# A hybrid layer and an expert layer on one core: more buffers for the RWKV keys, and TensorE's instructions held to the written order

## The chip, the cores and the metric

One core of a Trainium2 chip runs the whole program once. The metric is the device time of that execution in microseconds (us). TensorE is called PE here, VectorE DVE, ScalarE ACT, GpSimd POOL; SP is the engine that issues nearly all transfers.

## What is computed

Two layers follow each other on 2048 tokens of width 1024. The first is a hybrid layer: one projection `u = rmsnorm(x) @ w_in`, whose columns feed a gated linear attention (GLA, 4 heads) and an RWKV-7 recurrence (8 heads of 64), and one output projection. The second is a short convolution and 16 experts, each over 256 tokens. The change touches the RWKV part alone:

```python
def step(S, inp):                       # one token, per head; S is 64 x 64
    r_t, w_t, k_t, v_t, kk_t, a_t = inp
    sa = jnp.einsum('bhvk,bhk->bhv', S, -kk_t)
    S = (S * w_t[:, :, None, :]
         + sa[..., None] * (kk_t * a_t)[:, :, None, :]
         + v_t[..., None] * k_t[:, :, None, :])
    y = jnp.einsum('bhvk,bhk->bhv', S, r_t)
    return S, y
```

The kernel computes it in chunks of 64 tokens: products inside a chunk, the inverse of a small triangular matrix per head and chunk, and a state that goes from chunk to chunk.

## The kernel before

**The projection sets the pace.** `w_in` is multiplied in pieces of 128 columns by 512 tokens (four blocks of tokens, b = 0 to 3). Each weight and each activation is split in a high and a low part, so that one piece is 24 products of 128x128 by 512 columns (a depth of eight 128s, three products each): `dense` (line 85) issues 12 products, then calls `tick`, then 12 more and `tick` again. Products of this kind are called dense below. A piece of a block whose tokens have just been exchanged is written in two halves of 256 tokens (`proj`, line 356, product at line 384).

**The recurrence is written into the gaps.** `tick` ends a slot: it runs the steps that `plan` holds for that slot. A step is the stretch of a generator between two `yield`s; `yield n` puts the next stretch n slots later, and in a slot the steps of rank 0 come first, then 1, then 2. A block of 256 tokens (blk = 0 to 7) has two calls of `rwkv_prepare` (128 tokens each, 11 slots apart, rank 1) and one of `rwkv_chain` (rank 0, 27 slots after the block's start); blocks start 21 slots apart. There are 236 slots in all.

**`rwkv_prepare`** loads r, k, v, the decays `cs` and the keys' gates `ta` from DRAM. Two slots later it forms the keys `km` (from `ta` and k) and `rk`; three slots later PE sums `sq` and `rk` over each head (lines 1341, 1342, operand `hsel`) and DVE and POOL make the norm `nr`; three slots later the normed keys `kk`, the operands `ar`, and the scaled `ta` and `km`. Then PE turns `km`, `ta` and v token by token into `tks`, `tbs`, `tv` (three slots), and in the last two slots multiplies `ta` and `km` by `ar` (16 small products per chunk and operand pair, tile `rp`); DVE masks the results into `Ak`, `Ab0`, `Ab1`, and SP writes the two 32 x 32 triangles of `Ab0` to DRAM (`Ld`).

**`rwkv_chain`** loads the triangles, one per partition, and solves them on DVE: 31 steps j of two instructions each (lines 1436, 1438, tiles `PR` and `LX`), six steps to a slot. A copy (line 1441) and transfers through DRAM (`Xd`) bring the inverses into `TX` and `TM`; three slots later PE joins the halves (`pu<-TM,Ab`, then `pu<-TM,P`). Then each of four chunks takes three slots: state and values into `px`, `py`; `TX` times `WP` into `pu`; `U` into the state and the output.

**`decays`** (line 474, product at line 489) is the small projection of decays and gates: its first product `rp<-e,up` is written one slot after the piece that makes its operand e. **`modulation`** (line 125) is a side task in four sets of eight loads `araw`, summed by DVE into `acc` and by PE through `ahi`, `alo`. **`start_heads`** runs when all eight chains are written: it writes what is left of the modulation, and from then on two steps of the GLA heads go into each slot.

**What sets the order.** The program is not executed as written: a scheduler replays it with modelled times, gives each engine the oldest written instruction that the model takes as ready, and hands out a tile's buffers as they come free. Each engine then executes its list in that order. `burst` (line 1279) only holds the later products of a group behind its first.

Of the kernel before, what the change touches and what calls it, by code (L numbers as in the profile page):

```python
# [37 lines left out]

def bcast_rows(ap, n):

    return bass.AP(tensor=ap.tensor, offset=ap.offset, ap=[[0, 128], [1, n]])
# [3 lines left out]
def block_kernel(ctx: ExitStack, tc: tile.TileContext, A: dict, out: bass.AP, dbg=None, upto=99):  # L45
    nc = tc.nc
    dbg = dbg or {}
# [37 lines left out]
    def dense(ps, rhs, tick, parts):  # L85

        for k4 in range(0, KD, 4):
            hi, lo = parts()
            for k in range(4):
                rh, rl = rhs(k4 + k)  # L90
                nc.tensor.matmul(ps, hi[:, k, :], rh, start=(k4 + k == 0), stop=False)  # L91
                nc.tensor.matmul(ps, hi[:, k, :], rl, start=False, stop=False)  # L92
                nc.tensor.matmul(ps, lo[:, k, :], rh, start=False, stop=(k4 + k == KD - 1))  # L93
            tick()
# [56 lines left out]
    with ExitStack() as hps:  # L151
# [24 lines left out]
        def over_tokens():  # L176

            nw = rp.tile([1, D], F32, name="nw", tag="ar", bufs=3)
            nc.sync.dma_start(nw, A["norm_w"])
            one = rp.tile([1, 128], F32, name="one", tag="Ak", bufs=6)  # L180
            nc.vector.memset(one, 1.0)
            for c in range(0, D, 512):
                p = pst("mm", [128, 512], 2)
                nc.tensor.matmul(p, one, nw[:, c:c + 512], start=True, stop=True)
                nc.scalar.activation(nw_bc[:, c:c + 512], p, AF.Copy)
# [45 lines left out]
        def turned(tt):  # L231
# [4 lines left out]
            for g in range(2):  # L236
                p = pst("rp", [128, 4, 128], 3)
                for k in range(4):
                    nc.tensor.transpose(p[:, k, :], xr[:, (4 * g + k) * 128:(4 * g + k + 1) * 128], ident)
# [51 lines left out]
        nc.tensor.transpose(pv[:, :nv], vrow, ident[:nv, :nv])  # L291
# [40 lines left out]
        TX = cst.tile([128, 2, 4, 4, 64], F32)  # L332
# [23 lines left out]
        def proj(c0, at=""):  # L356
# [17 lines left out]
            else:  # L374
# [4 lines left out]
                for h in range(2):  # L379
                    hs = slice(h * 256, h * 256 + 256)  # L380
                    for k in range(KD):
                        hi, lo = (t[:, k % 4, :] for t in w[k // 4])
                        for l, r in ((hi, 0), (hi, 1), (lo, 0)):
                            nc.tensor.matmul(ps[:, hs], l, hT[r][:, k, hs], start=(k == 0 and l is hi and r == 0),
# [9 lines left out]
        def pair(c0, after=None):  # L394
# [3 lines left out]
            for k in range(KD):  # L398
# [6 lines left out]
                for o, w in zip(ps, ws):  # L405
                    hi, lo = (t[:, k % 4, :] for t in w)
                    for l, r in ((hi, 0), (hi, 1), (lo, 0)):
                        nc.tensor.matmul(o, l, hT[r][:, k], start=(k == 0 and l is hi and r == 0),
# [65 lines left out]
        def decays(b, e):  # L474
# [7 lines left out]
            for p in range(4):  # L482
# [3 lines left out]
                for i, (l, r) in enumerate(((0, eh), (0, el), (1, eh))):  # L486
                    for g in range(2):
                        rs = slice(64 * g, 64 * g + 64)
                        nc.tensor.matmul(ps[g], up[l][rs, c], r[rs], start=(i == 0), stop=(i == 2))
# [9 lines left out]
        def others(b, starts, after):  # L499
# [19 lines left out]
            for k in range(KD):  # L519
                nc.tensor.matmul(ps[0:32], gw[:, k, :], hT[0][:, k, :], start=(k == 0), stop=False,  # L520
                                 skip_group_check=True)
                nc.tensor.matmul(ps[0:16], gw[:, k, 0:16], hT[1][:, k, :], start=False,
# [21 lines left out]
        def gate_sums(b, ps):  # L544
# [6 lines left out]
            for g in range(2):  # L551
                pz = pst("mm", [128, TB], 2)
                nc.tensor.matmul(pz, gup[:, g * 128:g * 128 + 128], e, start=True, stop=True)
# [744 lines left out]
def rwkv_prepare(nc, blk, q, Ap, L):  # L1298

    rp, pst, ident, vcol = L["rp"], L["pst"], L["ident"], L["vcol"]  # L1300
# [13 lines left out]
    cs, ta = tmp("cs"), tmp("ta")  # L1314
# [15 lines left out]
    km = tmp("km")  # L1330
# [9 lines left out]
    for p in range(4):  # L1340
        nc.tensor.matmul(pn[:, 0, 2 * p:2 * p + 2], sq[:, p, :], hsel, start=True, stop=True)
        nc.tensor.matmul(pn[:, 0, 8 + 2 * p:10 + 2 * p], rk[:, p, :], hsel, start=True,
# [10 lines left out]
    for p in range(4):  # L1353
        nc.tensor.transpose(pb[:, p, :], nb[:, p, :], ident)
# [13 lines left out]
    for nme, s in (("ks", km), ("bs", ta), ("v", v)):  # L1368
        yield 2 if nme == "ks" else 1
        pT = pst("rp", T4, 3)  # L1370
        for p in range(4):
            nc.tensor.transpose(pT[:, p, :], s[:, p, :], ident)
        for c in range(2):
            tok[nme, c] = tmp("t" + nme, [128, 4, 64], 6)
# [4 lines left out]
        if nme == "v":  # L1379

            bo = tmp("bo", [128, 512], 3)
# [5 lines left out]
    for c in range(2):  # L1387
# [10 lines left out]
        burst(nc, L["tc"], products)  # L1398
        ent = {}
        ent["Ak"] = tmp("Ak", T4, 6)  # L1400
        nc.vector.tensor_mul(ent["Ak"], pA[0], amask[:, None, :].to_broadcast(T4))
        for a, bufs in ((0, 4), (1, 6)):
            ent["Ab" + str(a)] = tmp("Ab" + str(a), [128, 4, 64], bufs)
            cs_ = slice(64 * a, 64 * a + 64)
            nc.vector.tensor_mul(ent["Ab" + str(a)], pA[1][:, :, cs_],
                                 amask[:, None, cs_].to_broadcast([128, 4, 64]))
        for h in range(2):
            for bl in range(2):
                o = (1 - h) * 64 + bl * 32
                nc.sync.dma_start(Ld[blk % 2, bl, 2 * q + c, :, h].rearrange("p s t -> s p t"),  # L1410
                                  ent["Ab0"][o:o + 32, :, bl * 32:bl * 32 + 32])
# [4 lines left out]
def rwkv_chain(nc, blk, Ap, L):  # L1416

    rp, pst = L["rp"], L["pst"]
    S, TX, Ld, Xd = (L[n] for n in ("S", "TX", "Ld", "Xd"))
    orow, rsqrt, dbg, lnw_bc, tc = (L[n] for n in ("orow", "rsqrt", "dbg", "lnw_bc", "tc"))  # L1420
    T4 = [128, 4, 128]
    tmp, scr = rwkv_tiles(rp)
    TT = TX[:, blk % 2]
# [9 lines left out]
    for j in range(31):  # L1433
# [5 lines left out]
        if j % 6 == 5:  # L1439
# [30 lines left out]
    for c in reversed(range(4)):  # L1470
        for p in range(4):
            for o in (0, 64):
                products.append(((pP[o + 32:o + 64, c, p, :], Ap[c]["Ab0"][o:o + 32, p, 32:64],
                                  TM1(o)[:, :, 4 * c + p, :].rearrange("i o m -> i m o")),
                                 dict(start=True, stop=True)))
    burst(nc, tc, products)
# [13 lines left out]
    burst(nc, tc, products)  # L1490
# [7 lines left out]
    for c in range(4):  # L1498
# [13 lines left out]
        burst(nc, tc, products)  # L1512
# [12 lines left out]
        burst(nc, tc, products)  # L1525
# [4 lines left out]
        for p in range(4):  # L1530
            for o, w in ((pS, e["bs"]), (py, e["Ab1"])):
# [4 lines left out]
        burst(nc, tc, products)  # L1536
# [202 lines left out]
```

## Time and profile before

| | |
|---|---|
| median of 3 runs | 3367.67 us (3363.83 to 3373.88) |
| profiled execution, its own time | 3379.94 us |
| its span | 3378.0 us |
| PE busy | 3169.8 us (94%) |
| DVE, ACT, POOL busy | 64%, 41%, 15% |
| mean clock granted to PE, as a share of 2.4 GHz | 0.962 |

The span is the time from the first to the last instruction of the profiled execution. Busy is the time in which an engine worked on at least one instruction; a wait of an engine is put down to the instruction that released it. The granted clock is 1.00 at 2.4 GHz and 0.5 at 1.2 GHz; a number in between is a mean over a stretch.

### The profile page before, as it was taken

To read this page: it belongs to the slowest core of one execution; us is meant where nothing else is said; L and a number is where in the kernel's file an instruction comes from. 1 tells how busy PE (TensorE), PEld (TensorE's weight loads), DVE (VectorE), ACT (ScalarE), POOL (GpSimd) and SP (SyncE) were. 2 spreads that over 40 slices of the span, in tenths; PEclk is the share of its full clock that TensorE was granted. 3 is DMA by queue.
4 is the path that set the end of the run, shared out by engine and by line. 5 is a ranking of instruction groups with operands and counts; after the bars stand their busy time and mean duration, and the time that the engine had idled before them with its cause. 6 is when DMAs were issued, how large, how long until landed. Compare 5 with 4: busy or idle time off the path is not lost.

```text
span 3378.0 us, 56442 instructions
## 1 busy us (share of the span) xinstructions
PE 3169.8 (94%) x21579; PEld 2607.3 (77%) x21579; DVE 2146.5 (64%) x4292; ACT 1400.6 (41%) x2666; POOL 509.7 (15%) x534
## 2 busy tenths in 40 slices
PE   8898888998898799999999999959999999999998
PEld 6777767776676578878888888848888888888887
DVE  4565776567455775665443266578877777777765
ACT  4554545545343443331111123325555555555553
POOL 2332333322222111020000000020001100010000
PEclk9999888999899899999999999969999999999999
DMA  7555554555555775334421144336667766677665
GB/s 232 164 160 137 158 145 121 142 136 136 149 133 164 213 250 177 126 103 136 123 77 50 47 153 156 131 129 205 202 209 212 230 209 204 208 225 218 209 204 152
DMA packets 581936, 552.19 MB, mean 163 GB/s; under 512 B 106046, under 2 KB 466937, under 8 KB 581650
## 3 DMA queue, kind: packets, MB, share of 16 engines
q1 hardware_dynamic: 572188, 514.66, 49.9%
q0 software_dynamic: 9216, 33.56, 4.3%
q8 instruction: 170, 2.79, 0.3%
q14 instruction: 100, 0.82, 0.1%
q10 hardware_dynamic: 262, 0.36, 0.0%
HBM read 436.12 MB, written 112.35 MB: 162 GB/s over the span
## 4 chain that ended last, share of the span: by engine, by line
PE 75%; DVE 10%; DMA 5%; issue 3%; ACT 2%; SPq 1%; POOL 1%; POOLq 0%; DVEq 0%; ACTq 0%
PE mm L1236 14%; PE mm L1240 7%; PE mm L740 5%; PE mm L741 5%; PE mm L742 5%; PE mm L1267 3%; PE mm L1269 3%; PE mm L1268 3%; PE mm L91 2%; PE mm L92 2%; PE mm L93 2%; PE mm L908 2%; PE mm L909 2%; PE mm L910 2%; DVE LX L1438 1%
## 5 line engine op out<-in xcount | busy, mean ns | idle before, releaser
L74 ACT ACTIVATE whi<-wraw 128x1024 fp32r<-128x1024 f32 (+1 forms) x672 | 587.8, 877 | 986.8 <-PE mm L741 253.6
L76 DVE TENSOR_TENSOR wlo<-wraw,whi 128x1024 fp32r<-128x1024 f32 (+1 forms) x552 | 591.6, 1072 | 441.4 <-ACT whi L74 429.8
L1236 PE MATMUL mm<-xT,whi 128*128 128x512 f32 x2048 | 519.5, 395 | 0.6 <-DVE xT L1211 0.6
L1236 PEld LDWEIGHTS mm<-xT,whi 128*128 128x128 f32 x2048 | 367.8, 189 | 69.0 <-issue 3.2
L91 PE MATMUL mm<-hT,whi 128*128 128x512 f32 x768 | 324.1, 422 | 24.1 <-DVE ev L463 14.9
L93 PE MATMUL mm<-hT,wlo 128*128 128x512 f32 x768 | 315.8, 411 | 3.2 <-DVE wlo L76 2.9
L92 PE MATMUL mm<-hT,whi 128*128 128x512 f32 x768 | 316.8, 412 | 0.0
L740 PE MATMUL mm<-hlT,whi 128*128 128x512 f32 x768 | 300.1, 391 | 0.4 <-ACT hlT L640 0.4
L741 PE MATMUL mm<-hlT,whi 128*128 128x512 f32 x768 | 299.7, 390 | 0.0
L742 PE MATMUL mm<-hlT,wlo 128*128 128x512 f32 x768 | 299.2, 391 | 0.0
L1240 PEld LDWEIGHTS mm<-xT,wlo 128*128 128x128 f32 x2048 | 279.8, 190 | 20.2
L1240 PE MATMUL mm<-xT,wlo 128*128 128x256 f32 x2048 | 286.6, 282 | 0.0
L76 POOL TENSOR_TENSOR wlo<-wraw,whi 128x512 fp32r<-128x512 f32 (+1 forms) x120 | 166.5, 1389 | 392.7 <-ACT whi L74 316.8
L91 PEld LDWEIGHTS mm<-hT,whi 128*128 128x128 f32 x768 | 152.1, 198 | 67.3 <-DVE ev L463 18.6
L1267 PE MATMUL mm<-whi,hidT 128*128 128x512 f32 x512 | 201.1, 393 | 0.0
L1268 PE MATMUL mm<-wlo,hidT 128*128 128x512 f32 x512 | 200.3, 391 | 0.0
L1269 PE MATMUL mm<-whi,hidT 128*128 128x512 f32 x512 | 199.8, 390 | 0.0
L1273 POOL DMA_INDIRECT out_dram<-ys,idx x32 | 50.9, 1590 | 897.8 <-DVE ys L1271 892.9
L93 PEld LDWEIGHTS mm<-hT,wlo 128*128 128x128 f32 x768 | 152.3, 198 | 40.0 <-DVE wlo L76 5.4
L92 PEld LDWEIGHTS mm<-hT,whi 128*128 128x128 f32 x768 | 152.9, 199 | 31.7 <-issue 2.2
L740 PEld LDWEIGHTS mm<-hlT,whi 128*128 128x128 f32 x768 | 144.7, 189 | 31.7 <-ACT hlT L640 1.1
L741 PEld LDWEIGHTS mm<-hlT,whi 128*128 128x128 f32 x768 | 144.6, 188 | 30.3
(464 smaller groups left out, 5846.6 us busy)
## 6 DMA issues: line engine op xcount, KB each, us to landing
wraw<-in_moe_w_gate_dram SPq DMA_DIRECT2D x128, 512.0 KB
wraw<-in_moe_w_up_dram SPq DMA_DIRECT2D x128, 512.0 KB
wraw<-in_moe_w_down_dram SPq DMA_DIRECT2D x128, 512.0 KB
wraw<-in_w_in_dram SPq DMA_DIRECT2D x232, 256.0 KB
araw<-in_ada_w_dram SPq DMA_DIRECT2D x96, 256.0 KB
wraw<-in_sc_w_in_dram SPq DMA_DIRECT2D x56, 256.0 KB
mx<-ev SPq DMA_DIRECT2D x48, 256.0 KB
lr<-lat_d SPq DMA_DIRECT2D x24, 512.0 KB
```

The lines of the kernel that those rows point to most:

```text
L74: nc.scalar.activation(hi, raw, AF.Copy)
L76: eng.tensor_tensor(lo, raw, hi, op=OP.subtract)
L91: nc.tensor.matmul(ps, hi[:, k, :], rh, start=(k4 + k == 0), stop=False)
L92: nc.tensor.matmul(ps, hi[:, k, :], rl, start=False, stop=False)
L93: nc.tensor.matmul(ps, lo[:, k, :], rh, start=False, stop=(k4 + k == KD - 1))
L740: nc.tensor.matmul(o, hi, rh, start=(k == 0), stop=False)
L741: nc.tensor.matmul(o, hi, rl, start=False, stop=False)
L742: nc.tensor.matmul(o, lo, rh, start=False, stop=(k == KD - 1))
L1236: nc.tensor.matmul(pg[f], hi[:, k, f * 128:f * 128 + 128], xT[:, kk], start=(kk == 0), stop=False, skip_group_check=True)
L1240: nc.tensor.matmul(pg[f][:, 0], lo[:, k, f * 128:f * 128 + 128], xT[:, kk, 0], start=False, stop=(kk == KD - 1), skip_group_check=True)
L1267: nc.tensor.matmul(po[s], hT[0][:, k, ss], hi[:, i], start=(k == 0), stop=False)
L1268: nc.tensor.matmul(po[s], hT[0][:, k, ss], lo[:, i], start=False, stop=False)
```

## The change

Three things. First, a class `InOrder` ties every PE instruction that is issued through it to the PE instruction written just before it. The projection, the transposes, `decays`, `rwkv_prepare` and `rwkv_chain` go through it; the modulation's products and the GLA heads don't, so these may move ahead, but what is written behind them through `InOrder` may not pass them. Second, buffers: `ta` and `km` get 2 instead of 1, `tks`, `tbs`, `tv`, `Ak` and the second half of `Ab` 7 instead of 6, `bo` 4 instead of 3. `Ab0` (4 buffers of 64 columns) becomes `L0` (2 of 32) and `L1` (6 of 32), and the inverses `TX` have one buffer instead of two. Third, the triangular solve is cut at steps 3, 7, 11, 15, 20 and 25 instead of 5, 11, 17, 23 and 29, so that a chain takes one slot more.

```diff
+class InOrder:
+    def __init__(self, nc, tc):
+        self.eng, self.tc = nc.tensor, tc
+    def matmul(self, *args, **kw):
+        return self.tc.keep_in_program_order(self.eng.matmul(*args, **kw))
+    def transpose(self, *args, **kw):
+        return self.tc.keep_in_program_order(self.eng.transpose(*args, **kw))
...
-                nc.tensor.matmul(ps, hi[:, k, :], rh, start=(k4 + k == 0), stop=False)
+                pe.matmul(ps, hi[:, k, :], rh, start=(k4 + k == 0), stop=False)
...
-        TX = cst.tile([128, 2, 4, 4, 64], F32)
+        TX = cst.tile([128, 4, 4, 64], F32)
...
-def burst(nc, tc, products):
-    with ExitStack() as after:
-        for n, (args, kw) in enumerate(products):
-            m = nc.tensor.matmul(*args, **kw, skip_group_check=True)
-            if n == 0:
-                after.enter_context(tc.issue_after(m.ins))
+def burst(pe, products):
+    for args, kw in products:
+        pe.matmul(*args, **kw, skip_group_check=True)
...
-    cs, ta = tmp("cs"), tmp("ta")
+    cs, ta = tmp("cs"), tmp("ta", T4, 2)
...
-    km = tmp("km")
+    km = tmp("km", T4, 2)
...
-            tok[nme, c] = tmp("t" + nme, [128, 4, 64], 6)
+            tok[nme, c] = tmp("t" + nme, [128, 4, 64], 7)
...
-            bo = tmp("bo", [128, 512], 3)
+            bo = tmp("bo", [128, 512], 4)
...
-        ent["Ak"] = tmp("Ak", T4, 6)
+        ent["Ak"] = tmp("Ak", T4, 7)
...
-        for a, bufs in ((0, 4), (1, 6)):
-            ent["Ab" + str(a)] = tmp("Ab" + str(a), [128, 4, 64], bufs)
...
+        for a, o, n, bufs in (("L0", 0, 32, 2), ("L1", 32, 32, 6), ("Ab", 64, 64, 7)):
+            ent[a] = tmp(a, [128, 4, n], bufs)
+            nc.vector.tensor_mul(ent[a], pA[1][:, :, o:o + n], amask[:, None, o:o + n].to_broadcast([128, 4, n]))
...
-        if j % 6 == 5:
+        if j in (3, 7, 11, 15, 20, 25):
             yield 1
```

**Where instructions move: the keys on DVE.** DVE's list around one preparation in the middle of the stage. `Ak` is the last mask of the preparation before; `km`, `ta` and `rk` belong to the next one, and `nr` reads PE's sums over `rk`. Before:

```order
L1401 TENSOR_TENSOR Ak<-rp,amask 128x512
L1333 TENSOR_TENSOR km<-km,k 128x512
L1362 TENSOR_SCALAR ta<-ta 128x512
L1336 SCALAR_TENSOR_TENSOR rk<-r,vc,km 128x128 x4
L1436 TENSOR_TENSOR PR<-LX 128x31
L1365 TENSOR_TENSOR km<-km,En 128x512
L541 SCALAR_TENSOR_TENSOR ev<-ev,mm 128x512
```

and with the change, at the same place:

```order
L1411 TENSOR_TENSOR Ak<-rp,amask 128x512
L1570 TENSOR_TENSOR Y<-Y,bo 128x512
L1343 TENSOR_TENSOR km<-km,k 128x512
L1372 TENSOR_SCALAR ta<-ta 128x512
L90 TENSOR_TENSOR wlo<-wraw,whi 128x512
L1536 COPY U<-pu 128x256
L1355 TENSOR_SCALAR nr<-rp 128x8
L1356 COPY nr<-rp 128x8
L1445 TENSOR_TENSOR PR<-LX 128x31
```

Between the mask and the sums' reader `nr`, the products over `rk` no longer stand: `rk` has moved up, ahead of this stretch, and what follows `km` is the evacuation `U` and `nr` itself.

**Where instructions move: PE at the first heads.** PE's list where the GLA heads begin (`gv`, `kst`, `kin`, `gkt` are their operands, `pu` and `ss` the banks of the last dense pieces). Before, with 86 dense products written to `pu` and `ss` standing ahead of the first row of the heads:

```order
L91 MATMUL pu<-hT_99,whi 128x512
L92 MATMUL pu<-hT_100,whi 128x512
L1651 MATMUL rp<-ident,gv 128x128 x4
L1656 MATMUL rp<-ident,kst 128x128
L93 MATMUL pu<-hT_99,wlo 128x512
```

and with the change:

```order
L139 MATMUL mm<-ahi,ones 1x512
L140 MATMUL mm<-alo,ones 1x512
L139 MATMUL mm<-ahi,ones 1x512
L140 MATMUL mm<-alo,ones 1x512
L1660 MATMUL rp<-ident,gv 128x128 x4
L1665 MATMUL rp<-ident,kst 128x128
L1672 MATMUL rp<-qin,kin 128x128
L1665 MATMUL rp<-ident,kst 128x128
L1672 MATMUL rp<-qin,kin 128x128 x3
L1693 MATMUL rp<-gV,gkt 64x128 x8
L1660 MATMUL rp<-ident,gv 128x128 x4
L139 MATMUL mm<-ahi,ones 1x512
```

The modulation's last three pairs and the first heads have moved ahead of all 120 dense products of the banks `pu` and `ss`, which now follow the last `alo`.

## Rows read from the trace of the kernel before

**Rows 1.** The page: span, busy time by engine, granted clock in 40 slices.
```profile
span 3378.0 us, 56442 instructions
PE 3169.8 (94%) x21579; PEld 2607.3 (77%) x21579; DVE 2146.5 (64%) x4292; ACT 1400.6 (41%) x2666; POOL 509.7 (15%) x534
PEclk9999888999899899999999999969999999999999
```
**Rows 2.** Windows: length, busy time by engine, granted clock, DMA share, GB/s.
```profile
1200.00:1400.00 200.00, 200.00 (x1316) 163.44 (x1313) 129.82 (x275) 70.93 (x205) 23.75 (x30) 1.00 0.59 187
...
25.00:1175.00 1150.00, 1013.93 (x9996) 802.50 (x9996) 704.60 (x1523) 533.84 (x1058) 326.17 (x366) 0.92 0.56 154
...
1100.00:1175.00 75.00, 55.48 (x520) 42.54 (x520) 52.94 (x100) 30.86 (x69) 12.28 (x15) 0.89 0.67 203
```
**Rows 3.** Waits of PE, 20 to 1190 us: for what, total us, times, longest.
```profile
PE rp L1342 <- DVE rk L1336: 15.8, 9, 4.5
PE mm L91 <- DVE ev L463: 14.9, 9, 2.9
PE rp L1283 <- DVE Ak L1401: 13.2, 8, 3.3
PE ss L1283 <- DVE U L1527: 13.2, 6, 6.6
PE pu L1283 <- DMA TM<-Xd: 9.6, 4, 3.2
PE mm L91 <- DVE ev L556: 7.1, 4, 3.3
```
**Rows 4.** The tile `ta`, 200 to 1100 us: what its readers waited for.
```profile
  DMA ta<-wa_d: 36.2, 8
...
  DVE km L1333: 33.2, 12
```
**Rows 5.** DVE's groups, 200 to 1100 us.
```profile
L1438 DVE TENSOR_TENSOR LX<-LX,PR 128x126 f32<-128x126 f32 (+22 forms) x248 | 79.7, 321 | 5.8
L1436 DVE TENSOR_TENSOR PR<-LX 128x126 f32<-128x126 f32 (+22 forms) x248 | 78.4, 316 | 25.3 <-DMA LX<-Ld 19.5
...
L1405 DVE TENSOR_TENSOR Ab<-rp,amask 128x256 f32<-128x256 f32 x60 | 22.0, 414 | 5.9 <-PE pu L1283 5.8
L1401 DVE TENSOR_TENSOR Ak<-rp,amask 128x512 f32<-128x512 f32 x30 | 20.5, 682 | 1.1 <-PE rp L1283 1.0
```
**Rows 6.** PE's timeline: a dense product and the fifteenth after it (start us, us).
```profile
199.70 0.39 PE L93 MATMUL mm<-hT,wlo 128*128 128x512 f32 x1
...
203.11 0.40 PE L93 MATMUL mm<-hT,wlo 128*128 128x512 f32 x1
```
**Rows 7.** Timeline: the end of a piece, then its operand e made by ACT and DVE.
```profile
32.99 0.28 PE L384 MATMUL mm<-hT,wlo 128*128 128x256 f32 x1
...
37.56 0.62 ACT L478 ACTIVATE e<-ev 128x512 fp32r<-128x512 f32 x1
...
38.21 1.37 DVE L479 TENSOR_TENSOR e<-ev,e 128x512 fp32r<-128x512 f32 x1 [2.99 <-ACT e L478]
```
**Rows 8.** Timeline: the solve's last copy, and PE's products that wait for its way back.
```profile
261.57 0.62 DVE L1441 COPY LX<-LX 128x512 f32<-128x512 f32 x1
...
270.86 1.99 PE L1283 MATMUL pu<-TM,Ab 32*32 32x32 f32 x64 [1.59 <-DMA TM<-Xd]
```
**Rows 9.** PE's timeline at the end of the stage.
```profile
1104.26 0.39 PE L125 MATMUL mm<-ahi,ones 128*1 128x512 f32 x1
...
1112.11 0.37 PE L1283 MATMUL ss<-U,tbs 64*64 64x64 f32 x2 [6.61 <-DVE U L1527]
...
1115.98 1.12 PE L1283 MATMUL pu<-S,ar 64*64 64x64 f32 x16 [2.73 <-DVE S L1538]
...
1127.03 0.59 PE L125 MATMUL mm<-ahi,ones 128*1 128x512 f32 x1 [5.91 <-ACT ahi L120]
```
**Rows 10.** Windows of 25 us: idle and granted clock.
```profile
225.00:250.00 25.00, 23.69 (x133) 18.66 (x132) 21.74 (x60) 15.84 (x36) 8.30 (x8) 1.00 0.62 170
...
375.00:400.00 25.00, 15.95 (x283) 14.76 (x283) 18.13 (x35) 10.83 (x19) 9.33 (x11) 0.73 0.58 138
...
925.00:950.00 25.00, 25.00 (x265) 18.30 (x255) 19.67 (x55) 15.11 (x33) 7.83 (x9) 1.00 0.65 150
```

More of the change, by code (lines that the diff above doesn't have):

```diff
@@ L46, in block_kernel @@
     nc = tc.nc
+    pe = InOrder(nc, tc)
     dbg = dbg or {}
@@ L179, in over_tokens @@
             nc.sync.dma_start(nw, A["norm_w"])
-            one = rp.tile([1, 128], F32, name="one", tag="Ak", bufs=6)
+            one = rp.tile([1, 128], F32, name="one", tag="Ak", bufs=7)
             nc.vector.memset(one, 1.0)
@@ L183, in over_tokens @@
                 p = pst("mm", [128, 512], 2)
-                nc.tensor.matmul(p, one, nw[:, c:c + 512], start=True, stop=True)
+                pe.matmul(p, one, nw[:, c:c + 512], start=True, stop=True)
                 nc.scalar.activation(nw_bc[:, c:c + 512], p, AF.Copy)
@@ L383, in proj @@
                         for l, r in ((hi, 0), (hi, 1), (lo, 0)):
-                            nc.tensor.matmul(ps[:, hs], l, hT[r][:, k, hs], start=(k == 0 and l is hi and r == 0),
+                            pe.matmul(ps[:, hs], l, hT[r][:, k, hs], start=(k == 0 and l is hi and r == 0),
                                              stop=(k == KD - 1 and l is lo), skip_group_check=True)
@@ L407, in pair @@
                     for l, r in ((hi, 0), (hi, 1), (lo, 0)):
-                        nc.tensor.matmul(o, l, hT[r][:, k], start=(k == 0 and l is hi and r == 0),
+                        pe.matmul(o, l, hT[r][:, k], start=(k == 0 and l is hi and r == 0),
                                          stop=(k == KD - 1 and l is lo))
@@ L488, in decays @@
                         rs = slice(64 * g, 64 * g + 64)
-                        nc.tensor.matmul(ps[g], up[l][rs, c], r[rs], start=(i == 0), stop=(i == 2))
+                        pe.matmul(ps[g], up[l][rs, c], r[rs], start=(i == 0), stop=(i == 2))
                 for g in range(2):
@@ L552, in gate_sums @@
                 pz = pst("mm", [128, TB], 2)
-                nc.tensor.matmul(pz, gup[:, g * 128:g * 128 + 128], e, start=True, stop=True)
+                pe.matmul(pz, gup[:, g * 128:g * 128 + 128], e, start=True, stop=True)
                 az, mn, bias = ev(), ev(), vcol("gla_gate_bias", g)
@@ L1340, in rwkv_prepare @@
     for p in range(4):
-        nc.tensor.matmul(pn[:, 0, 2 * p:2 * p + 2], sq[:, p, :], hsel, start=True, stop=True)
-        nc.tensor.matmul(pn[:, 0, 8 + 2 * p:10 + 2 * p], rk[:, p, :], hsel, start=True,
+        pe.matmul(pn[:, 0, 2 * p:2 * p + 2], sq[:, p, :], hsel, start=True, stop=True)
+        pe.matmul(pn[:, 0, 8 + 2 * p:10 + 2 * p], rk[:, p, :], hsel, start=True,
                          stop=True)
@@ L1489, in rwkv_chain @@
                                  dict(start=True, stop=True)))
-    burst(nc, tc, products)
+    burst(pe, products)
     for h in range(2):
@@ L1524, in rwkv_chain @@
         products.insert(0, products.pop(2))
-        burst(nc, tc, products)
+        burst(pe, products)
         U = tmp("U", V4, 2)
@@ L1530, in rwkv_chain @@
         for p in range(4):
-            for o, w in ((pS, e["bs"]), (py, e["Ab1"])):
+            for o, w in ((pS, e["bs"]), (py, e["Ab"])):
                 for h, hs in enumerate(halves):
@@ L1535, in rwkv_chain @@
                                      dict(start=False, stop=True)))
-        burst(nc, tc, products)
+        burst(pe, products)
         nc.vector.tensor_add(S, pS, S)
```

37 lines of the change are left out of this document (17 added, 20 removed).

## Prediction

> **What bounds the kernel now.** I read the page first: PE is busy for 94% of the span, far ahead of every other engine, and its clock dips below full in the first third of the 40 slices more than anywhere else, apart from one slice near the middle [rows 1]. Then the windows: from 25 to 1175 us, the stage that the change touches, PE is idle for 1150.00 - 1013.93 = 136 us and its granted clock is 0.92, while from 1200 to 1400 us it is idle for nothing at 1.00 [rows 2]. So the stage is paced by PE, and what can be won there is PE's idle time and its lower clock; behind the stage the two orders differ little, and I put that at nothing, covered by a PE that is busy throughout.
>
> Then PE's waits in that stretch [rows 3]. They are many and short. The largest are for `rk` (15.8 us in 9 waits), for the evacuations `ev` that free the bank of a dense piece (14.9 and 7.1), for the masks `Ak` that free the banks `rp` (13.2), for `U` in the chain (13.2, half of it in one wait) and for `TM`, which comes through DRAM (9.6, in 4 of the 8 chains).
>
> **What a microsecond of idle time costs.** Between 25 and 1175 us the clock lost (1 - 0.92) x 1150 = 92 us beside 136 us of idle time [rows 2]: if all of that loss follows the waits, each one costs 0.68 us more; if none, nothing. Three windows stand for the pattern: with no idle time the clock was 1.00, with 1.3 us of it 1.00, with 9 us of it 0.73 [rows 10]. I take 0.5, three quarters of the upper bound, since a short wait cost no clock here. The Trainium skill (TensorE: Matmul & The Clock Gate, "A second HAM failure mode: psum-queue depth-cycling") says that short PE idles between groups, where PSUM banks cycle, are enough to make the clock swing. The rows agree in kind (0.73 beside 9 us of idle time), though not for the shortest waits. By the rule all of the loss would follow the waits, and the sum below would be -35 us and not -31.
>
> **The change, part by part.**
>
> *`ta` and `km` get a second buffer.* With one, the load of `ta` for the next preparation (11 slots on) has to wait for the last products that read it, in slots 13 and 14 of the one before; ACT then waits 36.2 us in total for it to land, and DVE 33.2 us for `km` [rows 4]. DVE's list shows the result: `km`, `ta`, `rk` right behind the last mask, and PE's sums soon after. With the change `rk` has moved up out of that place. So the wait for `rk` goes: **-15.8 us**. Bounds: 0, if it only waits for another load, to -15.8. What is late next on that path is `nr` on DVE, and its products stand three slots on.
>
> *PE keeps the written order: the banks `rp`.* A slot has 12 dense products; fifteen of them take 203.11 - 199.70 = 3.41 us [rows 6], so 12 take 2.7 us. The masks of one chunk take 0.68 + 2 x 0.41 = 1.5 us on DVE [rows 5]. As written, 12 dense products stand between the two chunks' groups, where the list of before often has fewer or splits a group. Bounds for the 13.2 us: 0 to -13.2. I take **-10**, near the upper one, since 2.7 covers 1.5 unless DVE is behind by over a microsecond.
>
> *The solve in smaller steps.* A step of the solve is 0.32 + 0.32 = 0.64 us on DVE [rows 5]; six to a slot are 3.8 us of DVE beside 2.7 us of dense products and what the slot's other steps add. Four or five are 2.6 to 3.2 us. DVE still does the same 62 instructions, but evacuations queue behind fewer of them. Of the 14.9 + 7.1 us of waits for `ev` I take **-8**; bounds 0 and -22.
>
> *Waits that the written order adds: e.* By PE's list the first product on e stood 36 dense products or more behind the piece that makes it; as written, 12. In the first block the piece ended at 32.99 + 0.28 = 33.3 us and the second part of e at 38.21 + 1.37 = 39.6 us [rows 7]: 6.3 us, less 2.7, leaves 3.6 us of wait in each of four blocks, 14 us. The lower bound is a path without queues: e's own two instructions, 2.0 us [rows 7], and three more of its kind before them at about 0.7 each, which is an estimate from the same rows' lengths, give 4.1 us and a wait of 1.4, that is 5 us. I take **+6**, near the lower end, because the first block also waits for its first weights. Behind the waiting product stands all of PE's list.
>
> *The same: `TM`.* The last copy of the solve began at 261.57 us and the products that need it at 270.86 [rows 8]: 9.3 us. As written, the copy's slot now holds five steps ahead of it (3.2 us), where it had one, and the products follow 36 dense products (8.2 us) and a few small ones. If DVE ran only as written, each of 8 chains would wait 3.2 + 9.3 - 8.2 = 4.3 us, 34 in all; in fact DVE runs ahead where operands allow, and 4 of 8 waited nothing. Bounds against the 9.6 us of before: -9.6 to +25. I take 16 us, hence **+6**.
>
> *The end of the stage.* Before, the last chunk of the last chain had no dense product between its groups: 6.61 and 2.73 us of waits, and 5.91 for the modulation [rows 9]. The dense pieces had been kept for later, where 86 of them (20 us) covered the loading of the first heads. As written, the chunk has its 12 dense products per step, and the heads have none: PE stops until the modulation's last sets are through. Two sets took 1127.03 - 1104.26 = 22.8 us [rows 9], under which lie 24 dense products (5.4 us); that leaves some 17 us, and a little more for the heads' own loads, against 75.00 - 55.48 = 19.5 us of idle time from 1100 to 1175 us before [rows 2]. I take **+1**; bounds -10 and +15.
>
> *At nothing:* the seventh buffer of `tks`, `tbs`, `tv`, `Ak`, `Ab` and the fourth of `bo` (no wait above names them; they only let ACT and DVE run further ahead), `L0` and `L1` for `Ab0` (the same columns in one more instruction per chunk, 32 in all at 0.41 us or less, beside a DVE that is busy 705 of 1150 us [rows 2]; without that cover 13 us), the single `TX` (its next load is written 29 slots after the one before, its last reader some 24), and the chain's extra slot (the last chain still ends before slot 236).
>
> **The sum:** -15.8 - 10 - 8 + 6 + 6 + 1 = -20.8; with the clock -20.8 x 1.5 = **-31 us**. The profiled execution took 3379.94 us, so it would take 3349; the median of the runs shown is 3367.67, 12 us less, so the forecast is **3337 us**. A measurement here can tell about 0.3%, 10 us, from no change.
>
> **Rivals.**
>
> *Slower: the written order stops PE where an operand comes late.* PE executed its list strictly in order: during the 6.61 us wait for `U` nothing else ran [rows 9]. The Trainium skill (TensorE: Matmul & The Clock Gate, "Part 3: Packing small matmuls — row/col tiling") states the same, that products start and end in program order; by it, every stop at a late operand stops all. For this rival speak the 9.3 us way back of the solve and e; against it that DVE and ACT, with more buffers, run ahead. Its place is `TM` and e: with `TM` at +25, e at +14, the end of the stage at +15 and only the `rk` wait gone, the sum is +38, with the clock +57: 3425 us. It decides from the point where these three cost more than the 34 us that I count as gains; at half of its price it is 3396. Chance 0.24.
>
> *Much faster: the buffers were all that was missing.* Then the waits inside the stage go together, and only those at loads that no buffer moves stay: of 136 us idle about 60 remain (the 19.5 at the end, and 40 in first loads and the ways through DRAM), -76, with all of the clock -128: 3240 us. The Trainium skill (Perfetto Trace Analysis, "Optimization Strategy") says that a gap which repeats on the engine that should be saturated can mean that there is no room for the next tile; by that rule the `ev` and `Ak` waits would go with the `rk` waits; no run so far shows it. Against it: `ev` and `Ak` free PSUM banks, and the change gives PSUM no buffer. Chance 0.12.
>
> *No change: the waits only change their names.* The `rk` wait is 15.8 us, and `TM` and e together take it back, or DVE, behind anyway, makes PE wait for `nr` in place of `rk`. The sum is within 10 us: 3368 us. Chance 0.16. That the change doesn't do what it says is no case: PE's list does stand as written up to the first heads.
>
> **How the numbers follow.** My forecast has 0.48, with a range of its own of 3297 to 3357. Faster: 0.48 + 0.12 = 0.60; same 0.16; slower 0.24. The range of 8 in 10 reaches up halfway into the slower rival, to 3396, which leaves about 0.1 above, and down to 3280, which leaves about 0.1 of the fast one below.
>
> **What would show it.** Right: no wait for `rk` among PE's first ten; the waits for `Ak` at a third or less; PE idle from 25 to 1175 us near 114 us and the clock at 0.93; waits of 1 to 4 us before the first product on e in each block, and a hole of 15 to 20 us before the first heads. Wrong: `rk` or `nr` still on top; `TM` waits of over 3 us in most chains; or idle time in the stage that is far under 100 us, which would say that the written order itself removed waits that I left in.

## The result, and the profile of the changed kernel

The changed kernel takes 3403 us (median of 4 runs, 3400 to 3410) against 3367 us before (4 runs): a ratio of 1.011, 95% interval 1.0096 to 1.0123. It is slower by 36 us, and the forecast was 3337. The profiled executions differ by 26 us (3406.04 against 3379.94). Their windows, to be held against [rows 2]; columns as there:

```profile
25.00:1175.00 1150.00, 987.64 (x10008) 779.40 (x10008) 703.05 (x1560) 531.95 (x1052) 325.74 (x367) 0.91 0.55 153
1100.00:1175.00 75.00, 52.62 (x283) 39.09 (x285) 49.05 (x96) 26.66 (x60) 13.03 (x16) 0.77 0.63 198
1200.00:1400.00 200.00, 200.00 (x1221) 158.46 (x1222) 119.22 (x258) 65.66 (x192) 20.88 (x27) 0.95 0.59 191
```

From 25 to 1175 us PE is idle for 162 us instead of 136. From 1200 to 1400 us it is idle for nothing, as before, but its granted clock is 0.95 instead of 1.00. PE's waits from 20 to 1190 us, to be held against [rows 3]:

```profile
PE ss L46 <- DVE U L1536: 25.8, 8, 6.7
PE rp L46 <- DVE Ab L1415: 22.8, 7, 5.7
PE mm L139 <- ACT ahi L134: 11.9, 2, 11.3
PE pu L46 <- DVE S L1547: 11.6, 5, 4.2
PE mm L46 <- DVE ev L570: 10.5, 4, 4.4
PE rp L1660 <- DMA gv<-gin: 10.0, 1, 10.0
...
PE mm L46 <- DVE ev L555: 9.4, 6, 2.8
PE pu L46 <- DMA TM<-Xd: 6.5, 5, 2.6
...
PE mm L46 <- DVE ev L477: 5.0, 4, 2.6
```

No wait for `rk` is left, but `U` stands at 25.8 us (13.2 before), and `Ab`, now the mask that PE waits for in the banks `rp`, at 22.8 (`Ak` 13.2 before).

**Where the time went.** Three points that both traces have cut the program: the last chain's `pu<-TM,P` (the second of its two groups on `TM`), the first `gv` of the heads, and the first product on `hlT`, which begins behind the output projection. By PE's lists 34 dense products fewer stand ahead of the first point now, and 86 fewer ahead of the second (2832 against 2918). At 0.227 us each (3.41 / 15, [rows 6]) this can be set off:

| stretch | before | after | dense products moved | change without them |
|---|---|---|---|---|
| 25 us to the last `pu<-TM,P` | 1035.3 us | 1021.4 us | -34, -7.7 us | **-6.2 us** |
| to the first `gv` | 92.1 | 82.7 | -52, -11.8 us | **+2.4** |
| to the first product on `hlT` | 272.4 | 320.8 | +86, +19.5 us | **+28.9** |

The first stretch, before and then after:

```profile
25.00:1060.29 1035.29, 922.01 (x9031) 732.48 (x9029) 635.18 (x1398) 483.31 (x957) 307.01 (x346) 0.92 0.55 151
```

```profile
25.00:1046.43 1021.43, 883.75 (x8999) 701.97 (x8997) 631.63 (x1428) 481.76 (x953) 304.30 (x345) 0.92 0.55 153
```

PE's idle time in it rose from 113 to 138 us, and the stretch is shorter all the same: PE's busy time fell by 38 us, of which the 34 products are 8. The clock is 0.92 in both. What took the other 30 us of busy time away was not followed up.

The third stretch is what the prediction had put at nothing. Its windows, before and then after:

```profile
1152.40:1424.80 272.40, 270.89 (x1800) 217.90 (x1799) 186.58 (x394) 108.41 (x301) 33.16 (x43) 1.00 0.62 199
```

```profile
1129.10:1449.90 320.80, 319.22 (x1887) 252.42 (x1888) 196.37 (x404) 114.52 (x312) 35.91 (x46) 0.93 0.55 179
```

PE is idle for 1.5 us of it before and for 1.6 after. Its clock is 1.00 before and 0.93 after: 0.07 x 320.8 = 22 of the 29 us are clock. The same in windows of 25 us, and the instructions in the middle of it (start us, us, then what ended the idle time):

```profile
1125.00:1150.00 25.00, 20.24 (x92) 15.43 (x93) 17.95 (x32) 12.14 (x23) 3.00 (x4) 0.63 0.81 259
1150.00:1175.00 25.00, 25.00 (x164) 18.91 (x165) 11.13 (x29) 7.69 (x25) 4.62 (x5) 1.00 0.43 127
1175.00:1200.00 25.00, 24.08 (x162) 17.93 (x163) 16.30 (x42) 13.08 (x44) 3.30 (x5) 0.83 0.62 190
1200.00:1225.00 25.00, 25.00 (x128) 18.34 (x129) 12.54 (x32) 8.11 (x29) 2.52 (x3) 0.62 0.67 224
1225.00:1250.00 25.00, 25.00 (x169) 18.43 (x168) 20.89 (x50) 11.33 (x36) 3.49 (x5) 1.00 0.69 228
```

```profile
1187.11 0.39 PE L46 MATMUL ss<-hT,wlo 128*128 128x512 f32 x1
1187.34 0.60 PE L1660 MATMUL rp<-ident,gv 128*128 128x128 f32 x4
...
1189.72 0.71 PE L1672 MATMUL rp<-qin,kin 64*128 64x128 f32 x4 [0.92 <-DVE gkt L1667]
1190.36 0.65 PE L1693 MATMUL rp<-gV,gkt 64*64 64x128 f32 x8
...
1194.90 1.11 PE L1660 MATMUL rp<-ident,gv 128*128 128x128 f32 x4
1195.94 1.12 PE L1688 MATMUL mm<-Sg,qin 64*64 64x128 f32 x8
...
1204.23 1.11 PE L670 MATMUL wy<-ident,o 128*128 128x128 f32 x4
```

The clock is lost in two places: some 9 us at the end of the hole at the heads and behind it (0.63 from 1125 to 1150), and, after a window at 1.00, some 14 us from 1175 to 1225 us, where PE stops for 0.92 us only. At 1187.11 the last dense product of the projection runs. Behind it PE has only products of 64 and 128 columns for 27 us, until the first long product of the output projection at 1214.39. Four transposes take 0.60 us at 1187.34 and 1.11 at 1194.90, and by the windows the clock stays at its lower level until about 1214.

Small products alone are not the reason. Behind the first `gv` more dense products run now than before (120 against 34). And before, too, PE had 17 us of small products between the last dense product (1167.05) and the first long one of the output projection (1184.67), with a wait of 0.96 us among them, at a clock of 1.00:

```profile
1167.40:1184.60 17.20, 16.24 (x160) 12.11 (x160) 13.08 (x37) 9.65 (x31) 1.87 (x3) 1.00 0.81 268
```

Why the clock fell after the change and not before is not shown. What is shown is the place and the price: the run free215 below, in which 86 more dense products stand ahead of the first `gv` again, has no hole there, has the clock back, and takes as long for the third stretch as the kernel before.

The hole itself came where it was forecast, 21 us long where 15 to 20 were forecast:

```profile
1117.81 0.59 PE L139 MATMUL mm<-ahi,ones 128*1 128x512 f32 x1 [11.26 <-ACT ahi L134]
...
1129.11 1.12 PE L1660 MATMUL rp<-ident,gv 128*128 128x128 f32 x4 [9.99 <-DMA gv<-gin]
```

### The profile page after: what moved, and what is told of

It is laid out like the page before. It is cut to its first block, busy times and chain, and to the rows that moved or that the text cites. A ratio compares the mean times of both kernels' runs of the same rounds, so it can differ in the third digit from the quotient of the medians.

```text
span 3404.2 us, 56548 instructions
## 1 busy us (share of the span) xinstructions
PE 3166.3 (93%) x21579; PEld 2599.1 (76%) x21579; DVE 2149.1 (63%) x4324; ACT 1399.4 (41%) x2666; POOL 504.9 (15%) x534
## 4 chain that ended last, share of the span: by engine, by line
PE 66%; DVE 2%; DMA 1%; issue 1%; ACT 1%; SPq 0%; POOL 0%; POOLq 0%; DVEq 0%; ACTq 0%
PE mm L1250 14%; PE mm L1254 7%; PE mm L754 5%; PE mm L755 5%; PE mm L756 5%; PE mm L1281 3%; PE mm L1283 3%; PE mm L1282 3%; PE mm L46 2%; PE mm L922 2%; PE mm L923 2%; PE mm L924 2%; PE mm L711 1%; PE mm L712 1%; PE mm L713 1%
## 5 line engine op out<-in xcount | busy, mean ns | idle before, releaser
L46 PE MATMUL mm<-hT,whi 128*128 128x512 f32 (+1 forms) x1888 | 611.4, 408 | 27.6 <-DVE ev L570 10.5
L46 PEld LDWEIGHTS mm<-hT,whi 128*128 128x128 f32 x1888 | 359.9, 203 | 110.8 <-DVE ev L570 11.5
L46 PE MATMUL mm<-hT,wlo 128*128 128x512 f32 (+1 forms) x944 | 374.3, 396 | 5.7 <-POOL wlo L90 3.3
L46 PEld LDWEIGHTS mm<-hT,wlo 128*128 128x128 f32 x944 | 190.1, 201 | 46.5 <-POOL wlo L90 4.8
L756 PEld LDWEIGHTS mm<-hlT,wlo 128*128 128x128 f32 x768 | 144.7, 188 | 30.2
L1283 PEld LDWEIGHTS mm<-whi,hidT 128*128 128x128 f32 x512 | 96.1, 188 | 20.1
```

The lines of the kernel that those rows point to most:

```text
L46: return self.tc.keep_in_program_order(self.eng.matmul(*args, **kw))
L756: nc.tensor.matmul(o, lo, rh, start=False, stop=(k == KD - 1))
L1283: nc.tensor.matmul(po[s], hT[1][:, k, ss], hi[:, i], start=False, stop=(k == KD - 1))
```

## The experiments

Each ratio is to runs of the kernel before on the same chip; differences between two kernels below are those of their ratios, times 3367 us.

| kernel | PE's order | buffers | cut | us | ratio (95% interval) |
|---|---|---|---|---|---|
| the change | held | new | new | 3403 | 1.011 (1.0096 to 1.0123) |
| only_buffers | free | new | new | 3358 | 0.9962 (0.9948 to 0.9976) |
| only_order | held | old | old | 3441 | 1.0212 (1.0195 to 1.0229) |
| old_cut | held | new | old | 3422 | 1.0157 (1.0140 to 1.0174) |
| one_ta | held | new, but one `ta`, `km` | new | 3442 | 1.0205 (1.0188 to 1.0222) |
| free215 | held to slot 215 | new | new | 3364 | 0.9986 (0.9975 to 0.9997) |
| free_heads | held to the heads | new | new | 3392 | 1.0068 (1.0050 to 1.0086) |
| mod2 | held | new | new | 3405 | 1.0105 (1.0087 to 1.0122) |
| lead2 | as free215 | new | new | 3375 | 1.0010 (0.9998 to 1.0022) |
| solve4 | as free215 | new | new | 3406 | 1.0094 (1.0077 to 1.0110) |
| held | as free215 | new | new | 3372 | 1.0010 (1.0001 to 1.0020) |
| buf_lead2 | free | new | new | 3358 | 0.9953 (0.9936 to 0.9969) |
| buf_held | free | new | new | 3341 | 0.9922 (0.9906 to 0.9939) |
| before_held | free | old | old | 3366 | 0.9993 (0.9983 to 1.0002) |

**The parts alone.** Buffers and cut without the order:

```diff
-        return self.tc.keep_in_program_order(self.eng.matmul(*args, **kw))
+        return self.eng.matmul(*args, **kw)
```

(the same for `transpose`; `burst` as before the change)

> The change with its buffers and the new cut of the solve, but no instruction of PE held to the written order. Order theory (holding PE to the written order is what costs): 3345 to 3368 us, at or below the kernel before (3367); PE's waits for rk gone, the first dense products in the banks pu and ss again ahead of the heads, no hole of 21 us at 1118 to 1139. Buffer theory (the second ta and km let ACT and DVE run up to a late load, and what stands behind them is late): over 3385 us, with PE's waits for U, S and Ab as large as after the change (26, 12 and 23 us).

The order alone is the diff of the change without its buffers and its cut.

> The kernel before with PE held to the written order alone: old buffers, old cut of the solve. Order theory: 3400 to 3440 us, since the wait for rk (15.8 us before) stays or grows and the hole before the first heads is there all the same. Buffer theory: 3355 to 3375, near the kernel before; the waits for U, S and Ab near those of before (13, 6, 13 us).

Released from slot 215 on:

```diff
     def keep(self, ins):
+        return self.tc.keep_in_program_order(ins) if self.on else ins
...
             slot[0] += 1
+            pe.on = slot[0] < 215
```

(`on` is True at first; once it is off, `burst` holds its products as before the change)

> The changed kernel, in which PE is released from the written order from slot 215 on (the last chain's chunks, the rest of the projection, the start of the heads). If the hole at the first heads is what the change lost: 3365 to 3380 us, 25 to 35 below the changed kernel's 3403, with PE's idle time between 1100 and 1150 us back under 15 us and the clock from 1100 to 1250 us at 0.92 or more. If the stage ahead of it lost as much (waits for U, S and Ab with the clock): 3385 to 3398 us.

With the old cut:

```diff
-        if j in (3, 7, 11, 15, 20, 25):
+        if j % 6 == 5:
```

> The changed kernel with the solve cut as before (six steps to a slot, a chain one slot shorter). If the finer cut and its extra slot cost nothing or help a little, as the prediction had it: 3400 to 3415 us. If the overlap of the next solve with the last chunk of a chain (which the extra slot makes longer) is what makes U and S late: 3385 to 3396 us, with the waits for U and S down by 10 us or more together.

The order is what costs: buffers and cut alone win (0.9962), the order alone loses 2.1%. only_buffers lies within the range of the order theory, only_order and free215 within 2 us of their first range. Of its loss on top of the buffers (1.011 - 0.9962, some 50 us) the release from slot 215 on gives back 1.011 - 0.9986, some 42 us; the stage before that slot holds some 8. The released kernel keeps 2918 dense products ahead of the first `gv`, as the kernel before does; its clock behind the stage is back, and its third stretch (1138.13 to 1410.45) is 272.3 us, against 272.4 before. The moved products set off, 29 of the 40 us between its profiled execution and that of the change lie there. The release frees all that PE does from slot 215 on, so the hole, the moved products and the clock are not told apart by it:

```profile
25.00:1175.00 1150.00, 999.82 (x10115) 787.90 (x10115) 715.56 (x1585) 539.62 (x1074) 330.44 (x370) 0.92 0.56 158
1175.00:1250.00 75.00, 75.00 (x550) 58.74 (x549) 57.75 (x138) 35.64 (x111) 11.09 (x12) 1.00 0.75 248
1200.00:1400.00 200.00, 200.00 (x1288) 164.38 (x1287) 127.30 (x257) 67.72 (x189) 22.81 (x31) 1.00 0.54 175
...
1138.13:1410.45 272.32, 270.23 (x1799) 217.42 (x1798) 187.27 (x394) 108.19 (x301) 33.97 (x43) 1.00 0.60 200
```

The expectation on the old cut fell: it is some 16 us slower (1.0157 against 1.011), not faster, so the finer cut helps under the order. It takes PE's waits from one name to another. With the old cut:

```profile
PE rp L46 <- DVE Ab L1415: 34.2, 13, 5.7
PE pu L46 <- DMA TM<-Xd: 30.4, 7, 9.2
...
PE ss L46 <- DVE U L1536: 9.6, 6, 3.2
```

`TM` falls from 30.4 to 6.5 us and `Ab` from 34.2 to 22.8, while `U` rises from 9.6 to 25.8. Without the order, too, `U` stands at 26.1 us in 13 waits with the new cut (only_buffers).

**The second `ta` and `km`.** One buffer each, all else as changed:

```diff
-    cs, ta = tmp("cs"), tmp("ta", T4, 2)
+    cs, ta = tmp("cs"), tmp("ta")
```

(`km` likewise)

> The changed kernel with one buffer each for ta and km, as before; the other buffers, the cut and the order stay. Holding PE to the written order alone made the wait for rk 69 us, the finer cut is worth 19 us and all buffers together another 18. If it is the second ta and km that take the rk wait away: 3415 to 3435 us with PE's wait for rk at 40 us or more. If the other buffers do it: 3400 to 3410 us with no wait for rk.

PE's wait for `rk`, with the order alone and then with one `ta`:

```profile
PE rp L46 <- DVE rk L1346: 69.2, 15, 9.2
```

```profile
PE rp L46 <- DVE rk L1346: 71.5, 14, 9.8
```

With PE held, the wait for `rk` is 70 us and not 16, as nothing that is written behind the waiting product may be put ahead of it in PE's list; the second `ta` and `km` remove all of it, and are worth some 32 us under the order (1.0205 against 1.011). The wait is as the first case had it, the time above its range. Without them nothing else of the change helps against the order (1.0205 against 1.0212).

**Is it the modulation, or the passing of the heads?** A modulation step after more pieces, and a release only at the heads:

```diff
-            if slot[0] % 6 == 0:
+            if slot[0] % 2 == 0:
```

> The changed kernel, every PE instruction in the written order up to the first heads, with a step of the modulation after each piece that allows it and not after every third, so that the modulation is through before the heads begin. If the modulation's last sets make the hole of 21 us at the first heads: no wait for ahi at the heads, 3370 to 3385 us. If the heads' own loads alone make it as long (the wait for gv grows from 10 to some 20 us): 3393 to 3405 us.

```diff
         def start_heads():
+            pe.on = False
```

> The changed kernel, released from the written order only when the heads begin. Released from slot 215 on it took 39 us less, but that release also lets dense products of the last chain's slots fall behind the heads' first steps: 2918 of them stand ahead of the first gv there, 2832 in the changed kernel, 2844 here. If what counts is work kept back from the last chain's slots: 3393 to 3405 us, with waits for ahi and gv of 15 us or more together at the first heads. If what counts is only that dense products may pass the modulation and the heads: 3362 to 3378 us.

With the modulation done early the wait for `ahi` at the heads is gone, but waits of 10.3 us for an `ev` and of 11.1 for a `whi` stand elsewhere, and the time is the same; the modulation's part of the hole is not told apart by this. The wait for `gv` is 11.8 us, so neither case holds, though the time lies in the range of the second. The release at the heads lets 12 dense products move and gives back some 14 us of the 42, with 8.8 us for `ahi` and 9.5 for `gv` left, as the first case of its expectation had it (its time is a microsecond below the range). So the rest of the 42 hangs on what is released between slot 215 and the heads; that this is the 74 further dense products is likely and not tested by itself.

**What makes `U` late.** In several of its long waits DVE stood before something else, with `U` behind it. DVE from 538 us, ACT at the same time, and PE:

```profile
538.78 0.68 DVE L1411 TENSOR_TENSOR Ak<-rp,amask 128x512 f32<-128x512 f32 x1
543.21 0.69 DVE L1343 TENSOR_TENSOR km<-km,k 128x512 f32<-128x512 f32 x1 [3.76 <-ACT km L1342]
...
544.16 0.42 DVE L1536 COPY U<-pu 128x256 f32<-128x256 f32 x1
```

```profile
532.73 0.37 ACT L1523 ACTIVATE WP<-pu 128x256 f32<-128x256 f32 x1
541.54 1.65 ACT L1342 ACTIVATE km<-ta,oka,half 128x128 f32<-128x128 f32 x4 [8.43 <-DMA ta<-wa_d]
```

```profile
544.63 0.37 PE L46 MATMUL ss<-U,tbs 64*64 64x64 f32 x2 [5.00 <-DVE U L1536]
```

`km` waits for ACT, ACT for the load of `ta`, and `U` is ready 5 us late. This `km` is not of the preparation whose `nr` comes next on DVE, as the list of the changed kernel was read above: by the trace that one's `km` and `rk` ran at 508.57 and 519.36 us, its `nr` at 582.80, and the `km` at 543.21 belongs to the preparation after it (`rk` at 597.61). The second buffer lets it stand that far ahead. Two tries on top of the release from slot 215 followed from it, loads two slots earlier and two more slots ahead of the solve:

```diff
-                        run(rwkv_prepare(nc, blk, q, Ap, locals()), s + 11 * q, 1)
+                        t = max(slot[0], s + 11 * q - 2)
+                        lead = s + 11 * q - t
+                        run(rwkv_prepare(nc, blk, q, Ap, locals()), t, 1)
...
-    yield 2
+    yield 2 + L["lead"]
```

> The kernel released from slot 215 on, in which the five loads of a preparation are written two slots earlier. Theory that U and Ab are late because ACT and DVE stand before the load of ta, which SP issues late: ACT's wait for ta (71.6 us in the changed kernel) under 35 us, PE's waits for U and Ab together (55 us in the kernel released from slot 215) under 35 us, 3335 to 3355 us. Rival (DVE is late for its own work, and the load only changes what it stands before): ACT's wait falls, U and Ab stay within 10 us, 3357 to 3368 us.

```diff
         nc.gpsimd.memset(X[64 * o:64 * o + 64].rearrange("u i m -> u (i m)")[:, 16 * o:512:33], 1.0)
-    yield 2
+    yield 4
```

> The kernel released from slot 215 on, with four slots and not two between the loads of the triangles LX and the solve. If U and S are late because DVE stands before LX with U behind it: DVE's wait for LX (30.3 us in the changed kernel) under 12 us, PE's waits for U and S (45 us together) down by 10 us or more, 3345 to 3358 us. If not: 3360 to 3372 us, the chain being two slots longer.

The same lead in the kernel without PE's order:

> Buffers and the new cut without the order, with the five loads of a preparation written two slots earlier. If late loads are what is left of the waits also without the order: 3335 to 3352 us, below the 3358 of the same without the lead. If the scheduler has already put the loads as early as buffers allow: 3354 to 3362 us.

The first two missed both of their cases, and the third came out as its second case (3358 us, no gain). With the lead ACT's wait for `ta` is 81.5 us: the loads are issued within 5 us of where they stood without it. Eleven of fourteen follow within 9 us on the last product that reads `ta` for the preparation two before (it starts at 166.28 us, the load is issued at 168.56), so what most of them wait for is the buffer, not the slot. The kernel is some 8 us slower than without the lead, which is not explained. Two more slots ahead of the solve only bring DVE's wait for `LX` from 30.4 to 20.1 us, and PE's waits for `U` and `S` rise from 45 to 58 us; a new wait of 22.8 us, for `ar`, stands beside them, and the kernel is some 36 us slower (1.0094 against 0.9986), which is not explained either. Then ACT's key steps were tied to their slots, with PE released from slot 215 on, without PE's order, and in the kernel before:

```diff
+    keep = L["tc"].keep_in_program_order
-    nc.scalar.activation(En, cs, AF.Exp, scale=-1.0)
+    keep(nc.scalar.activation(En, cs, AF.Exp, scale=-1.0))
```

(likewise `Ep`, `sq`, ACT's `km` and DVE's `km`)

> The kernel released from slot 215 on, in which ACT's first steps of a preparation (Ep, En, sq, km) and DVE's product km also keep the written order, so that they can't be placed ahead of their slot, where they stand before the load of ta. Writing the loads earlier left ACT's wait for ta at 82 us, because a load of ta begins only when the products of the preparation two before have freed its buffer. If early placing is what makes U late: ACT's wait for ta under 25 us, PE's waits for U and S (45 us) down by 12 us or more, 3340 to 3358 us. If not: 3360 to 3375 us, U and S within 8 us.

> Buffers and the new cut, PE's instructions not held, but ACT's first steps of a preparation and DVE's km in the written order. If early placing costs here too (ACT waits 38 us for ta, PE 26 us for U): 3335 to 3352 us. If not: 3355 to 3368 us.

> The kernel before, with its single ta and km and the old cut, in which only ACT's first steps of a preparation (Ep, En, sq, km) and DVE's product km keep the written order. Buffers and cut without PE's order gave 3358 us, with these steps held 3341. If the hold is a gain of its own: 3345 to 3358 us here too. If it pays only because a second ta and km let the steps be placed early: 3362 to 3385 us, with PE's wait for rk at 15 us or more.

ACT no longer waits for `ta` in either kernel with two of them. With PE's order that wins nothing (1.0010 against 0.9986): `U` and `S` stand at 24.6 and 22.9 us, together 47.5 against 45.2, so early keys are not what makes them late there; DVE's wait for `LX` rises from 30.4 to 52.2 us. Without the order it wins some 13 us (0.9922 against 0.9962), and this version, 3341 us, beats both kernels, but not by `U`:

```profile
PE ss L1297 <- DVE U L1541: 28.6, 10, 5.1
```

The waits for `hT` and `nb` (13.3 and 8.9 us in only_buffers) have left the top, and PE is idle for 117 us from 25 to 1175 us instead of 138. In the kernel before the hold wins nothing (though its wait for `rk` is 10.7 us, under the 15 of that case), so its gain needs the new buffers or the new cut; which of them is not told apart. What makes `U` late in general stays open: its long waits have `km`, the solve's `LX`, `wlo` or the modulation's `acc` ahead of it on DVE, and no one of them accounts for most.

## Why the prediction was wrong

The step that failed is in its first part: "behind the stage the two orders differ little, and I put that at nothing, covered by a PE that is busy throughout". PE is busy throughout, and the stretch costs 28.9 us, 22 of them by a clock of 0.93 instead of 1.00. It is about half of the miss: of the 57 us between the 3349 that were forecast for the profiled execution and the 3406 that it took, 29 lie there, 27 in the stage ahead, whose terms follow below, and 1 between the two. A busy PE was read as a PE that gets its work done, after [rows 10], where no idle time went with a clock of 1.00; the window from 1200 to 1225 us has no idle time and 0.62. By the rule of the Trainium skill that the prediction weighed (TensorE: Matmul & The Clock Gate, "A second HAM failure mode: psum-queue depth-cycling") the clock swings with short idles of PE. It does not decide here: the first 9 us follow waits of 11.26 and 9.99 us, which are not short, 14 us more were lost behind one wait of 0.92 us, and a wait of 0.96 us at the same place cost no clock before. What brought the clock down stays open.

*The end of the stage, +1 (bounds -10 and +15).* The hole was right: 11.3 and 10.0 us of waits, and idle time from 1100 to 1175 us up by 2.9 us. But the term stopped at the hole. The prediction had the 86 kept dense products and counted them as 20 us of cover; what follows behind a hole that is not covered was not asked. Released from slot 215 on, which keeps them, the kernel is some 42 us faster.

*The stage ahead of it, -21.8, with the clock -33.* It gained 6.2 us by the table above, and not by its terms: they add up waits, and PE's idle time rose by 24 us where 22 less were forecast, while 30 us of busy time went that no term has. The price of 0.5 us of clock for each microsecond of idle time did not hold either: the clock is 0.92 with 113 us of idle time and with 138. Term by term:

- `rk`, -15.8: right, all of it went. That the order would have made it 70 us without the second buffers was not seen.
- `rp` banks, -10: wrong by sign. `Ak` 13.2 became `Ab` 22.8, in 7 waits. DVE is behind by more than the microsecond that the step allowed; at 714 us it worked through the solve and `wlo` ahead of the masks:

```profile
712.13 0.69 DVE L90 TENSOR_TENSOR wlo<-wraw,whi 128x512 fp32r<-128x512 f32 x1
712.74 0.27 DVE L1447 TENSOR_TENSOR LX<-LX,PR 128x108 f32<-128x108 f32 x1
713.03 0.26 DVE L1445 TENSOR_TENSOR PR<-LX 128x96 f32<-128x96 f32 x1
713.33 0.26 DVE L1447 TENSOR_TENSOR LX<-LX,PR 128x96 f32<-128x96 f32 x1
713.50 0.48 DVE L1415 TENSOR_TENSOR L<-rp,amask 128x128 f32<-128x128 f32 x2
713.90 0.42 DVE L1415 TENSOR_TENSOR Ab<-rp,amask 128x256 f32<-128x256 f32 x1
```

```profile
714.46 0.48 PE L46 MATMUL rp<-ar,km 64*64 64x128 f32 x2 [5.68 <-DVE Ab L1415]
```

- `ev`, -8: near in size, by luck. The two rows that it named (lines 477 and 570 now) fell from 22.0 to 15.5 us; with the third `ev` (line 555) it is 24.9 against 36.0. But the finer solve is not what did it: in those two rows the order alone has 2.7 us, the order with the old cut 7.8, and the new cut without the order 29.1.
- `e`, +6: right, 4.6 us (3.5 for ACT's part, 1.1 for DVE's), in three of the four blocks.
- `TM`, +6: too high, -3.1 (6.5 us in 5 waits). The cut, credited to `ev`, paid here: with the old one it is 30.4 us, near the bound of 34 that was worked out for a DVE that runs only as written.
- `U` and `S`, not in the sum: together from 18.9 to 37.4 us, +18.5. They are late operands like `TM` and e, at the place where PE has 12 dense products (2.7 us) between a group and its reader. ACT's `P` is another: 9.6 us in 2 waits, none before.
- At nothing: the other buffers, as far as one_ta tells, which has them and gains nothing by them and the cut. The chain's extra slot is not told apart: the run with the old cut, which lacks it, changes both and is slower.

Of its own marks, no wait for `rk`, the short waits for e (in three blocks) and, at 21 us, the hole held; the masks at a third, 114 us of idle time (162) and a clock of 0.93 (0.91) did not.

The rival that forecast the side, "the written order stops PE where an operand comes late", was right in its mechanism: the rule that it leaned on (same page of the Trainium skill, "Part 3: Packing small matmuls — row/col tiling") agrees with the 5.00 us before `U` at 544.63 and, above all, with `rk` at 69 us under the order against 15.8. Its place was wrong: `TM` and e cost 1.5 us together and not 39. That 3403 lies between its half price (3396) and its full one (3425) is luck; no rival had the stretch behind the heads. The rival "the buffers were all that was missing" has the run only_buffers against it: the waits for `ev` and `U` did not go with `rk`. The rule named there (Trainium skill, Perfetto Trace Analysis, "Optimization Strategy"), that a repeating gap can mean no room for the next tile, fits `rk` alone: PE's wait for it fell from 71.5 us with one `ta` to none with two. The run gained 13 us and not 128.

## What to carry to other kernels

Ask of work that a scheduler has put off what it covers and what runs behind it: the release that puts 20 us of long products ahead of the heads again went with a gain of some 42 us. Price a hole on the saturated engine by what runs for the next hundred microseconds, and look at the granted clock where that engine is "busy". Do not take a sum of waits for the time: the stage had 24 us more of them and was not longer. An order held on one in-order engine makes each late operand of any other engine its own stop, so hold it only where its operands are early, and let it go before the stretch where the work runs out. Here no kernel with the order held was faster than the same without it (1.011, or 0.9986 with the release, against 0.9962).

## What the hardware showed beyond that

- PE at its lower clock while busy without a gap: from 1195 to 1214.3 us it has 19.30 us of busy time and a clock of 0.50, with products of 64 and 128 columns alone:

```profile
1195.00:1214.30 19.30, 19.30 (x106) 14.07 (x106) 10.46 (x27) 7.53 (x27) 1.57 (x2) 0.50 0.87 287
```

- Products of the same kinds, without a long one among them, went at 1.00 in the kernel before from 1167.40 to 1184.60 us (row above). In solve4, where 45 us pass without a long product (1169.34 to 1214.34), the clock was first at the lower level, behind 2.9 us of idle time, and then back at the upper one:

```profile
1175.00:1195.00 20.00, 19.99 (x117) 14.35 (x118) 10.69 (x28) 9.96 (x32) 1.20 (x2) 0.50 0.79 254
1200.00:1205.00 5.00, 4.13 (x39) 2.98 (x39) 4.47 (x11) 3.78 (x14) 0.00 (x0) 1.00 0.84 227
```

- So a run of small products went at either level, and neither the busy time nor the length of the products tells by itself which. What does stays open.
